# Low halves from GpSimd to VectorE, one activation kept in program order, and rotations issued by ScalarE, in a hybrid mLSTM and sparse-attention block

## The chip, the cores and the metric

The kernel runs on one core of one Trainium2 chip. The metric is the device time of one execution in microseconds (us); lower is better. The kernel before was timed in three runs with a median of 608.86 us.

## What is computed

One layer of a decoder block on 512 tokens of width 1024, in float32. The part of the reference that the change touches:

```
hN = _rmsnorm(x, norm_g[l])
p = _split_in(hN @ w_in[l])
...
kc = _compress(kvh(p["n_kc"]), cmp_pos_k[l], cmp_w1_k[l], cmp_w2_k[l])
vc = _compress(kvh(p["n_vc"]), cmp_pos_v[l], cmp_w1_v[l], cmp_w2_v[l])
ks = _partial_rope(kvh(p["n_ks"]), positions).transpose(0, 2, 1, 3)
kw = _partial_rope(kvh(p["n_kw"]), positions).transpose(0, 2, 1, 3)
...
return jax.nn.gelu(blocks @ w1) @ w2
```

The last line is the end of `_compress`. The queries are rotated with `_partial_rope` too. Behind this come an attention over 8 heads with three branches, the mLSTM over 4 heads, gates, two branch projections, an output projection, a residual sum and a final norm.

## The kernel before

Matrix products run in float32 precision as three passes on TensorE: each operand is split into a high half (a rounded copy, mostly made by ScalarE) and a low half (the operand minus the high half, mostly made by VectorE), and high times high, high times low and low times high are summed in PSUM. Names that end in `h` and `l`, or `hi` and `lo`, are such halves. So every weight that arrives costs a ScalarE copy (`wh<-wr`) and a VectorE subtraction (`wl<-wr,wh`) before the third pass of its product can start.

The stages that matter here, in order of time:

1. **Keys** (to 28 us). Raw columns of x (`xc`) times the weights of four key and value projections, into four PSUM banks (`keys_in`, L484). Beside it the norm's factor is worked out (`rs`) and spread over a tile `rB`.
2. **Small projection** (28 to 44 us). For each of 8 row blocks k, `normed_raw` (L509) makes the normed columns in place (`xc<-xc,rB`, VectorE), ScalarE makes the high half `hTh`, and `normed_low` (L512) makes the low half `hTl` (VectorE). `small(i)` (L504) makes the halves `shi` (ScalarE) and `slo` (GpSimd, `pool` in the code) of the narrow weights `sraw`, two row blocks at a time. TensorE takes, for each k, 12 matmuls of 288 columns (L624), of which the last four need `hTl` of that k; 96 in all. After the fourth k, the four key and value sums are moved out of PSUM (`kc`, `vc`, `ks`, `kw`), and the rotations of `ks` and `kw` are sent.
3. **Streamed jobs** (44 to about 90 us). A `Stream` feeds TensorE with jobs: gate projections, query projections (24 matmuls of 512 columns each, L230, L232, L234) and the first layers of the compression (8 matmuls, L277). Raw weights sit in three buffers `wr`; the next load is issued when a buffer has been split. In between come `keys(b)` (L344), which rotates the keys of branch b and makes their halves; `blocks(i)` (L719), which lays the keys and values out for the compression (tiles `Z`); `hidden(i)` (L739), the compression's activation, a chain of two small matmuls, a copy `ua` on ScalarE, four small VectorE steps, a tanh on ScalarE (`ub<-ub`) and two VectorE steps that end in `u`; and `compress_k`, whose matmul (L758) needs `u`.
4. **Attention** (about 90 to 230 us), with streamed jobs between the scores, then the mLSTM and the projections.

A rotation swaps 8-row strips of a tile into `rot`, by four small DMAs of 8 x 512 (`rotate`, L317 to L320). The keys' two rotations are issued by SyncE and GpSimd, the four of the queries (`rope_a`, L689) by SyncE, in `turned`, which the stream calls when the next job begins.

The order on the engines comes from two places. Where `ordered` names an engine (`act`, `dve`, `pool`), its instructions stay as the program issues them; elsewhere a scheduler of the framework places them. In stages 1 and 2 `act` and `dve` are ordered; `hidden` is not. Each engine executes its own list strictly in order, so an instruction that waits holds up all behind it.

Of the kernel before, what the change touches and what calls it, by code (L numbers as in the profile page):

```python
# [11 lines left out]
F32 = mybir.dt.float32  # L12
F32R = mybir.dt.float32r
I32 = mybir.dt.int32
AF = mybir.ActivationFunctionType
OP = mybir.AluOpType
AX = mybir.AxisListType.X

T = 512
# [70 lines left out]
def build(  # L90
# [3 lines left out]
    nc = tc.nc  # L94
    ordered = {"act", "dve"}

    class Engine:
# [15 lines left out]
    act, dve, pool = (  # L113
        Engine(e, n) for e, n in ((nc.scalar, "act"), (nc.vector, "dve"), (nc.gpsimd, "pool"))
    )
    A = act.activation
# [13 lines left out]
    def f(ap):  # L130
        return ap.bitcast(F32)
# [55 lines left out]
    class Stream:  # L187
# [27 lines left out]
        def run(self, jobs=1):  # L215
            for _ in range(jobs):
                self.step(1)
                while self.cur is not None:
                    self.step(1)
# [69 lines left out]
    prm = cst[:, CEND:CPOS].rearrange("p (c n) -> p c n", c=8)  # L289
# [16 lines left out]
    rpp = rp.__enter__()  # L306
# [10 lines left out]
    def rotate(rot, r, queue):  # L317
        for o in (0, 64):
            queue.dma_start(rot[o : o + 8], r[o + 8 : o + 16])
            queue.dma_start(rot[o + 8 : o + 16], r[o : o + 8])  # L320
# [3 lines left out]
    def turn_keys(b):  # L324
        rotate(turned_keys[b], kv[2 + b], nc.gpsimd if b else nc.sync)
# [9 lines left out]
    away, kv = {}, {}  # L335
# [8 lines left out]
    def keys(b):  # L344
        k = kv[2 + b]
        dve.tensor_tensor(k, k, Ct, OP.mult)
        rope_b(k, turned_keys[b])
        for g in range(2):
            s = slice(g * 64, g * 64 + 64)
            kh, kl = KK[g][0][s, b], KK[g][1][s, b]  # L350
            A(kh, k[s], AF.Copy)
            pool.tensor_tensor(kl, k[s], f(kh), OP.subtract)
        for g in range(2 * b):
            s = slice(g * 64, g * 64 + 64)
            o = slice((1 - g) * 64, (1 - g) * 64 + 64)
            for t in KK[g]:
                doubled.append(lambda t=t, o=o, s=s: nc.sync.dma_start(f(t[o]), f(t[s])))
# [18 lines left out]
    with tc.tile_pool(name="small", bufs=1, side="right") as sp, tc.tile_pool(  # L376
        name="ph0", bufs=2, side="right"
# [5 lines left out]
        raw = sp.tile([128, ND, SW], F32, name="sraw")  # L383
        shi = sp.tile([128, ND, SW], F32R, name="shi")
        slo = sp.tile([128, ND, SW], F32R, name="slo")
# [9 lines left out]
        rB = rpp.tile([128, T], F32, name="rB", tag="z", bufs=1)  # L395
# [59 lines left out]
        def x_low(k):  # L455
            dve.scalar_tensor_tensor(xl[k], xv[k], gv[k], f(xh[k]), OP.mult, OP.subtract)
# [11 lines left out]
        keys_in = [PP(), PP(), PP(), PO()]  # L468

        def kv_step(k):  # L470
            a, b = wh[k // 2][:, k % 2], wl[k // 2][:, k % 2]
            todo = [(p, c) for p in range(3) for c in range(4)]
            if k == 5:
                todo.insert(6, None)
            if k == ND - 1:
                todo = [(p, c) for c in range(4) for p in range(3)]
            for what in todo:
                if what is None:
                    factors()
                    continue  # L480
                p, c = what
                cs_ = slice(c * 128, c * 128 + 128)
                pin(
                    pe.matmul(  # L484
                        keys_in[c], (b if p == 2 else a)[:, cs_], xl[k] if p == 1 else xh[k],
                        start=k == 0 and p == 0, stop=k == ND - 1 and p == 2,
                    )
                )
# [12 lines left out]
            x_low(k)  # L501
            w_low(k // 2, slice(k % 2, k % 2 + 1), dve if k > 1 else pool)

        def small(i):  # L504
            ks = slice(2 * i, 2 * i + 2)
            A(shi[:, ks], raw[:, ks], AF.Copy)
            pool.tensor_tensor(slo[:, ks], raw[:, ks], f(shi[:, ks]), OP.subtract)

        def normed_raw(k):  # L509
            dve.scalar_tensor_tensor(xv[k], xv[k], gv[k], rB, OP.mult, OP.mult)  # L510
# [1 line left out]
        def normed_low(k):  # L512
            dve.tensor_tensor(hTl[:, k], xv[k], f(hTh[:, k]), OP.subtract)
# [21 lines left out]
        def sines():  # L535
            A(sc, ang, AF.Sin)
            for j, (i, sign) in enumerate(((1, 1.0), (1, 1.0), (0, -1.0), (0, 1.0))):
                pool.tensor_scalar(turned4[:, j], sc[:, i], sign, 1.0, OP.mult, OP.mult)
            nc.sync.dma_start(table.rearrange("j p t -> p j t"), turned4)
            turns4 = table.rearrange("j (f g) t -> (j f) (g t)", f=8)  # L540
            for dst, o in ((Ct, 0), (St, 16)):
                for g in (0, 64):
                    nc.sync.dma_start(dst[g : g + 16], turns4[o : o + 16])
# [41 lines left out]
        x_low(6)  # L585
        w_low(3)
        kv_step(5)
        A(rB, pr, AF.Copy)
        x_high(7)
        act.preload_act_table_set("silu_and_others")  # L590
        sines()
        normed_raw(0)
        x_low(7)
        kv_step(6)
        kv_step(7)

        for k in range(ND):
            if k < 4:
                small(k)
            A(hTh[:, k], xv[k], AF.Copy)  # L600
            if k < ND - 1:
                normed_raw(k + 1)
            normed_low(k)
            if k == 3:
                dve.tensor_scalar(prm[:, :, 10], prm[:, :, 10], 0.5, None, OP.mult)
                for c, (n, tag, bufs) in enumerate(
                    (("kc", "slt", 1), ("vc", "rw", 1), ("ks", "Th0", 2), ("kw", "Th1", 2))
                ):
                    kv[c] = rpp.tile([128, T], F32, name=n, tag=tag, bufs=bufs)
                    dve.tensor_tensor(kv[c], keys_in[c], rB, OP.mult)  # L610
                    if c > 1:
                        turn_keys(c - 2)
        stream.ahead = 1
        stream.fetch()
        stream.ahead = 2
        for b in range(2):
            keys(b)
        accs = [PS(), PS(), PT(), PT()]

        def project(k, tb, p):  # L620
# [68 lines left out]
    def rope_a(ps, name):  # L689
        r = rpp.tile([128, T], F32, name="rw", tag="rw", bufs=1)  # L690
        a = rpp.tile([128, T], F32, name="ra", tag="ra")
        A(r, ps, AF.Copy)
        dve.tensor_tensor(a, ps, Ct, OP.mult)
        rot = ropes.popleft()
        hl = [rpp.tile([128, T], F32R, name="r" + n, tag="r" + n) for n in "hl"]
        split(ps, *hl)

        def turned():
            rotate(rot, r, nc.sync)
            roped[name] = *hl, a, rot  # L700

        stream.then.append(turned)

    cmp_pool = tc.tile_pool(name="cmp", bufs=1, side="right")
# [14 lines left out]
    def blocks(i):  # L719
        z, parts = Z[i], []  # L720
        for g in range(2):
            for p in range(2):
                src = kv[i][g * 64 : g * 64 + 64, :].rearrange("p (n j b) -> p j n b", n=32, b=2)
                parts.append((src[:, :, :, p], *(z[p * 64 : p * 64 + 64, 0, :, l, g] for l in range(2))))
        for src, hi, lo in parts:
            A(hi, src, AF.Copy)
        for src, hi, lo in parts:
            dve.tensor_tensor(lo, src, f(hi), OP.subtract)
        rows = z.rearrange("p c j l g n -> p c (j l g) n")
        A(rows[:, 1, :, 0:31], f(rows[:, 0, :, 1:32]), AF.Copy)  # L730
        for c in range(2):
            o = i * 16 + c * 8
            for g in range(2):
                A(
                    z[:, c, :, :, g, 31].rearrange("p j l -> p l j"), f(cpos2[:, :, o : o + 8]),
                    AF.Copy,
                )

    def hidden(i):  # L739
        ph = PS()  # L740
        pe.matmul(ph[:, :64], first[i][:, 0], both, start=True, stop=False)
        pe.matmul(ph[:, :64], first[i][:, 1], both, start=False, stop=True)
        u0 = cp.tile([128, 64], F32, name="ua", tag="ua")
        u = cp.tile([128, 64], F32, name=f"u{i}")
        u2 = cp.tile([128, 64], F32, name="ub", tag="ub")
        A(u0, ph[:, :64], AF.Copy)
        dve.tensor_scalar(u, u0, u0[:, 31:32], None, OP.add)
        dve.tensor_tensor(u2, u, u, OP.mult)
        dve.tensor_scalar(u2, u2, 0.044715, 1.0, OP.mult, OP.add)
        dve.tensor_tensor(u2, u2, u, OP.mult)  # L750
        A(u2, u2, AF.Tanh, scale=float(np.sqrt(2 / np.pi)))
        dve.tensor_scalar(u2, u2, 0.5, 0.5, OP.mult, OP.add)
        dve.tensor_tensor(u, u, u2, OP.mult)
        return u
# [187 lines left out]
    A(gates, gp[:, :, 0:24], AF.Tanh, scale=0.5)  # L942
    pool.tensor_scalar(gates, gates, 0.5, 0.5, OP.mult, OP.add)
    run()
    run()
    stream.step(1)
    stream.ahead = 3
# [2 lines left out]
    for _ in log_forget():  # L950
        stream.step(1)
    stream.step(5)
    u0 = hidden(0)
    stream.step(8)
    stream.then.extend(doubled)
    stream.run(2)
# [5 lines left out]
    for_head(0)  # L962
    for_head(1)
    ordered.clear()
    u1 = hidden(1)
    stream.step(14)
    compress_v(u1)
    trig_pool.__exit__(None, None, None)
# [180 lines left out]
    n = 0  # L1149
# [403 lines left out]
    for h in range(4):  # L1553
# [5 lines left out]
        for sb in range(NT):  # L1559
            o, n = KOFF[sb], 512 - sb * 128  # L1560
# [41 lines left out]
        r = rsqrt(mp, va, NT, "rl")  # L1602
# [342 lines left out]
```

## Time and profile before

| what | value |
|---|---|
| median of 3 runs | 608.86 us (607.76 to 609.02) |
| profiled execution, time | 608.19 us |
| profiled execution, span from first to last instruction | 606.4 us |
| TensorE busy | 587.8 us (97%) |
| VectorE busy | 462.2 us (76%) |
| ScalarE busy | 363.7 us (60%) |
| GpSimd busy | 128.0 us (21%) |
| DMA moved | 129.52 MB, mean 214 GB/s |

In the views, PE is TensorE, PEld its weight load, DVE is VectorE, ACT is ScalarE, POOL is GpSimd and SPq is SyncE's queue. A row of the timeline gives the start, the duration, the engine, the line, the operation, the output and inputs, and in brackets how long the engine had been idle and what ended that. Ends of matmuls are modelled, so a wait of TensorE is best read from the starts. In a row of the windows, each engine's busy time is followed by its number of instructions in brackets; PEclk is the TensorE clock that was granted, as a share of full speed. L105 is the line of a helper through which nearly all VectorE, ScalarE and GpSimd instructions pass.

### The profile page before, as it was taken

How to read it: one execution, taken by the hardware profiler on the slowest of the kernel's cores; microseconds unless marked ns; L12 is line 12 of the kernel's file. 1: busy time of each engine (PE TensorE's matmuls, PEld its weight loads, DVE VectorE, ACT ScalarE, POOL GpSimd, SP SyncE). 2: the span in 40 equal slices, each digit the busy share in tenths (PEclk: the TensorE clock that was granted, in tenths of full speed). 3: DMA queues.
4: the chain of work that ended last, by engine and by line, in shares of the span. 5: the costliest groups of instructions: out<-in, count | busy, mean ns of one | idle time of the engine just before them, and what ended most of it. 6: DMA issues, size and time to landing. Idle time of an engine off the chain costs nothing.

```text
span 606.4 us, 8551 instructions
## 1 busy us (share of the span) xinstructions
PE 587.8 (97%) x2896; PEld 491.9 (81%) x2896; DVE 462.2 (76%) x855; ACT 363.7 (60%) x662; POOL 128.0 (21%) x204
## 2 busy tenths in 40 slices
PE   9989979998999999999999999999999999999995
PEld 6887768877878888888888888888888888888884
DVE  4799669867778778777999745869777766679885
ACT  6747755656657666665766666565756542644544
POOL 5634052335314534250000000000200010001011
PEclk9999989999999999999999999999999999999999
DMA  8936962876994799489684456699995697867723
GB/s 320 329 96 197 260 172 76 265 159 129 259 324 139 172 200 240 140 211 225 206 273 143 138 168 185 181 310 332 300 269 181 218 249 247 294 199 253 249 98 140
DMA packets 102484, 129.52 MB, mean 214 GB/s; under 512 B 6052, under 2 KB 63012, under 8 KB 102312
## 3 DMA queue, kind: packets, MB, share of 16 engines
q1 hardware_dynamic: 96392, 113.83, 59.3%
q0 software_dynamic: 5760, 14.75, 14.1%
q8 instruction: 23, 0.38, 0.3%
q10 hardware_dynamic: 288, 0.39, 0.2%
q14 instruction: 21, 0.17, 0.1%
HBM read 110.66 MB, written 42.02 MB: 252 GB/s over the span
## 4 chain that ended last, share of the span: by engine, by line
PE 79%; DVE 8%; ACT 5%; DMA 5%; issue 1%; SPq 1%; DVEq 0%; ACTq 0%
PE pp L232 11%; PE pp L234 10%; PE pp L230 10%; PE pp L1331 3%; PE pp L1333 3%; PE pp L1335 3%; PE pt L1069 2%; PE pp L484 2%; PE pt L1333 2%; PE pt L1335 2%; PE pt L1331 2%; PE pp L1673 2%; PE pp L1669 2%; PE pp L1671 2%; PE po L1081 1%
## 5 line engine op out<-in xcount | busy, mean ns | idle before, releaser
L105 DVE TENSOR_TENSOR wl<-wr,wh 128x1024 fp32r<-128x1024 f32 (+3 forms) x105 | 125.2, 1192 | 53.3 <-ACT wh L105 52.0
L105 ACT ACTIVATE wh<-wr 128x1024 fp32r<-128x1024 f32 (+3 forms) x106 | 108.0, 1021 | 79.1 <-PE pp L232 24.6
L234 PE MATMUL pp<-hTh,wl 128*128 128x512 f32 x320 | 126.6, 396 | 0.4 <-DVE wl L105 0.4
L232 PE MATMUL pp<-hTl,wh 128*128 128x512 f32 x320 | 126.5, 395 | 0.0
L230 PE MATMUL pp<-hTh,wh 128*128 128x512 f32 x320 | 126.2, 394 | 0.0
L105 POOL TENSOR_SCALAR P<-P,st,gates 128x128 f32<-128x128 f32 (+2 forms) x80 | 52.6, 681 | 107.1 <-DVE st L105 95.7
L234 PEld LDWEIGHTS pp<-hTh,wl 128*128 128x128 f32 x320 | 60.4, 189 | 12.7 <-DVE wl L105 1.2
L230 PEld LDWEIGHTS pp<-hTh,wh 128*128 128x128 f32 x320 | 60.5, 189 | 11.3
L232 PEld LDWEIGHTS pp<-hTl,wh 128*128 128x128 f32 x320 | 60.5, 189 | 11.2
L105 ACT ACTIVATE P<-P,st 128x128 f32<-128x128 f32 (+3 forms) x64 | 35.7, 559 | 31.3 <-DVE st L105 30.7
L105 POOL TENSOR_TENSOR rlr<-va,mhalf 128x4 f32<-128x4 f32 x4 | 4.1, 1034 | 222.3 <-ACT Dm L105 150.6
L105 DVE SCALAR_TENSOR_TENSOR u<-pp,cst,u 128x511 f32<-128x511 f32 (+2 forms) x48 | 35.6, 741 | 5.7 <-ACT u L105 5.5
L105 DVE CUSTOM_DVE_ANT_0 P<-ps,cst 128x128 f32<-128x128 f32 (+3 forms) x64 | 30.0, 478 | 8.0 <-PE ps L1050 5.8
L105 DVE TENSOR_TENSOR ptl<-pt,pth 128x384 fp32r<-128x384 f32 (+1 forms) x48 | 28.4, 592 | 5.7 <-ACT pth L105 5.7
L105 ACT ACTIVATE pth<-pt 128x384 fp32r<-128x384 f32 (+1 forms) x48 | 25.0, 520 | 11.9 <-PE pt L1069 11.4
L1069 PE MATMUL pt<-cst,P 128*128 128x128 f32 x160 | 25.6, 273 | 1.6 <-DVE ptl L105 1.6
L1069 PEld LDWEIGHTS pt<-cst,P 128*128 128x128 f32 x160 | 19.9, 140 | 6.1 <-DVE ptl L105 2.6
L1080 PE MATMUL po<-pth,vsw 128*128 128x512 f32 (+1 forms) x64 | 21.8, 350 | 0.7 <-DVE oc L105 0.7
L1081 PE MATMUL po<-ptl,vsw 128*128 128x512 f32 (+1 forms) x64 | 19.3, 328 | 0.0
L1335 PE MATMUL pp<-wh,S 128*128 128x512 f32 x48 | 18.7, 389 | 0.0
L1331 PE MATMUL pt<-wh,S 128*128 128x512 f32 x48 | 18.7, 389 | 0.0
L1333 PE MATMUL pt<-wl,S 128*128 128x512 f32 x48 | 18.7, 389 | 0.0
(429 smaller groups left out, 1415.6 us busy)
## 6 DMA issues: line engine op xcount, KB each, us to landing
wr<-w_in SPq DMA_DIRECT2D x62, 512.0 KB
qk<-hl SPq DMA_DIRECT2D x16, 512.0 KB
qk<-qk SPq DMA_DIRECT2D x16, 512.0 KB
wsumv<-w_in SPq DMA_DIRECT2D x4, 1024.0 KB
away<-s SPq DMA_DIRECT2D x16, 256.0 KB
wsumz<-w_in SPq DMA_DIRECT2D x4, 1024.0 KB
wsumout<-w_out SPq DMA_DIRECT2D x4, 1024.0 KB
wr<-wsumv SPq DMA_DIRECT2D x8, 512.0 KB
```

Of the source, the lines that this page charges most:

```text
L105: ins = fn(*args, **kw)
L230: pe.matmul(ps, a, c, start=k == 0, stop=False)
L232: pe.matmul(ps, a, d, start=False, stop=False)
L234: pe.matmul(ps, b, c, start=False, stop=k == nk - 1)
L484: pe.matmul(keys_in[c], (b if p == 2 else a)[:, cs_], xl[k] if p == 1 else xh[k], start=k == 0 and p == 0, stop=k == ND - 1 and p == 2,)
L1069: pe.transpose(pt[:, n : n + 128], P[:, POFF[qb] + kb * 128 : POFF[qb] + kb * 128 + 128], ident)
L1080: pe.matmul(po[:, kb * 128 :], vl, th, start=b == 0 and kb == 0, stop=False)
L1081: pe.matmul(po[:, kb * 128 :], vl, tl, start=False, stop=False)
L1331: pe.matmul(ps, a, c, start=begin, stop=False, skip_group_check=not first)
L1333: pe.matmul(ps, a, d, start=False, stop=False, skip_group_check=not first)
L1335: pe.matmul(ps, b, c, start=False, stop=k == 3, skip_group_check=not first)
L1669: pe.matmul(ps, p, ya(k), start=k == 0, stop=False)
```

## The change

Four edits:

- **Low halves.** The four `slo` subtractions go from GpSimd to VectorE, each behind the normalizations of one row block (`small_low`); the `shi` copies move up by a block, the first ahead of `rB`. The four low halves of the keys (`kl` in `keys`) go from GpSimd to VectorE as well. The table load for the sines, and the sines, move behind the second `shi`.
- **Order of the keys.** `ks` and `kw` are moved out of PSUM after row block 3 as before, `kc` and `vc` only after the loop (`keys_out`). `keys(1)` moves behind the first streamed job.
- **Activation in order.** `hidden(0)` and `hidden(1)` are issued with `act` and `dve` ordered (`in_order`).
- **Rotations of the queries.** `rope_a` calls `rotate` itself, on ScalarE's queue, instead of later on SyncE's.

```
             A(kh, k[s], AF.Copy)
-            pool.tensor_tensor(kl, k[s], f(kh), OP.subtract)
+            dve.tensor_tensor(kl, k[s], f(kh), OP.subtract)
...
-            pool.tensor_tensor(slo[:, ks], raw[:, ks], f(shi[:, ks]), OP.subtract)
...
+        def small_low(i):
+            dve.tensor_tensor(slo[:, pairs[i]], raw[:, pairs[i]], f(shi[:, pairs[i]]), OP.subtract)
...
+        small_high(0)
         A(rB, pr, AF.Copy)
         x_high(7)
-        act.preload_act_table_set("silu_and_others")
-        sines()
         normed_raw(0)
         x_low(7)
+        small_low(0)
...
+        def keys_out(c):
+            n, tag, bufs = (("kc", "slt", 1), ("vc", "rw", 1), ("ks", "Th0", 2), ("kw", "Th1", 2))[c]
+            kv[c] = rpp.tile([128, T], F32, name=n, tag=tag, bufs=bufs)
+            dve.tensor_tensor(kv[c], keys_in[c], rB, OP.mult)
+            if c > 1:
+                turn_keys(c - 2)
...
         for k in range(ND):
-            if k < 4:
-                small(k)
             A(hTh[:, k], xv[k], AF.Copy)
+            if k < 3:
+                small_high(k + 1)
+            if k == 0:
+                act.preload_act_table_set("silu_and_others")
+                sines()
             if k < ND - 1:
                 normed_raw(k + 1)
             normed_low(k)
+            if k < 3:
+                small_low(k + 1)
             if k == 3:
...
+                keys_out(2)
+                keys_out(3)
...
-        for b in range(2):
-            keys(b)
+        keys_out(0)
+        keys_out(1)
+        keys(0)
...
         def turned():
-            rotate(rot, r, nc.sync)
             roped[name] = *hl, a, rot
 
+        rotate(rot, r, nc.scalar)
         stream.then.append(turned)
...
+    def in_order(fn, *args):
+        ordered.update({"act", "dve"})
+        out = fn(*args)
+        ordered.clear()
+        return out
...
     run()
+    keys(1)
     run()
...
-    u0 = hidden(0)
+    u0 = in_order(hidden, 0)
...
-    u1 = hidden(1)
+    u1 = in_order(hidden, 1)
```

VectorE's list at the start of the small projection; `Th_143` is the last low half of x for the keys, and the rest are named above:

```order
 L105 SCALAR_TENSOR_TENSOR xc<-xc,rB 128x512
 L105 SCALAR_TENSOR_TENSOR Th_143<-xc,k_111 128x512
+L105 TENSOR_TENSOR slo<-sraw,shi 128x576
 L105 SCALAR_TENSOR_TENSOR xc<-xc,rB 128x512
 L105 TENSOR_TENSOR hTl<-xc,hTh 128x512
+L105 TENSOR_TENSOR slo<-sraw,shi 128x576
 L105 SCALAR_TENSOR_TENSOR xc<-xc,rB 128x512
 L105 TENSOR_TENSOR hTl<-xc,hTh 128x512
```

A `slo` now stands ahead of each of the second to fifth `xc<-xc,rB`. GpSimd's list loses its four.

ScalarE's list at the first activation of the compression; `ft` belongs to the forget gate, `s` to a gate job, `wh` are the high halves of the weights of coming jobs, `h` is the second first-layer sum, `KC` the compressed keys, `Th` the halves of the rotated queries. Numbers tell the `wh` apart:

```order
 L105 ACTIVATE ft_792<-ft_792 128x16
-L105 ACTIVATE wh_866<-wr_864 128x1024
 L105 ACTIVATE ua_840<-ps_837 128x64
+L105 ACTIVATE ub_842<-ub_842 128x64
 L105 ACTIVATE wh_886<-wr_884 128x1024
-L105 ACTIVATE ub_842<-ub_842 128x64
 L105 ACTIVATE s_861<-pp_802 128x512
 L105 ACTIVATE wh_912<-wr_910 128x1024
-L105 ACTIVATE Th_921<-ra_717 64x512
 L105 ACTIVATE h_898<-ps_875 128x256
```

The tanh `ub` now stands directly behind `ua`, ahead of `wh_886`; `wh_866` has moved up, ahead of this piece. On VectorE the subtraction for `wh_886` likewise moved from ahead of the last two steps of `u` to behind them.

ScalarE's list where the second query projection is moved out of PSUM, early in the attention; `rw` is the tile that is rotated, `rh` its unrotated high half, `P` a softmax block:

```order
 L105 ACTIVATE rh<-pp 128x512
+L319 DMA rot_88<-rw 8x512
+L320 DMA rot_88<-rw 8x512
+L319 DMA rot_88<-rw 8x512
+L320 DMA rot_88<-rw 8x512
 L105 ACTIVATE P,st<-P,st 128x256
 L105 ACTIVATE sc<-sc 128x256
```

Four DMA issues now stand in ScalarE's list ahead of the next softmax block; SyncE's list loses the same four. For the third query projection they stand ahead of a `pth<-pt` copy, the high half of transposed probabilities, and for the fourth behind a `wh<-wr`.

More of the change, by code (lines that the diff above doesn't have):

```diff
@@ L502, in both_low, with small_high @@
             w_low(k // 2, slice(k % 2, k % 2 + 1), dve if k > 1 else pool)
-        def small(i):
-            ks = slice(2 * i, 2 * i + 2)
-            A(shi[:, ks], raw[:, ks], AF.Copy)
-            pool.tensor_tensor(slo[:, ks], raw[:, ks], f(shi[:, ks]), OP.subtract)
+        pairs = [slice(2 * i, 2 * i + 2) for i in range(4)]
+        def small_high(i):
+            A(shi[:, pairs[i]], raw[:, pairs[i]], AF.Copy)
+        def small_low(i):
+            dve.tensor_tensor(slo[:, pairs[i]], raw[:, pairs[i]], f(shi[:, pairs[i]]), OP.subtract)
         def normed_raw(k):
@@ L603, in build @@
             normed_low(k)
+            if k < 3:
+                small_low(k + 1)
             if k == 3:
[L605 to L612, printed above, removed]
+                keys_out(2)
+                keys_out(3)
+        dve.tensor_scalar(prm[:, :, 10], prm[:, :, 10], 0.5, None, OP.mult)
         stream.ahead = 1
```

## The prediction

> **What bounds the kernel now.** I read the page's busy times first. TensorE (PE) has work nearly all the time.
>
> ```profile
> PE 587.8 (97%) x2896; PEld 491.9 (81%) x2896; DVE 462.2 (76%) x855; ACT 363.7 (60%) x662; POOL 128.0 (21%) x204
> ```
>
> So a gain is a gap on PE that closes. The windows by stage show where the gaps are: the columns are length, busy time of PE, PEld, DVE, ACT and POOL, then the granted clock, the DMA share and GB/s.
>
> ```profile
> 28.20:43.90 15.70, 13.60 (x98) 13.02 (x97) 15.34 (x21) 7.21 (x10) 6.36 (x7) 1.00 0.38 105
> 43.90:60.00 16.10, 15.89 (x71) 12.86 (x70) 15.75 (x26) 12.15 (x27) 7.89 (x7) 1.00 0.66 187
> 60.00:72.00 12.00, 11.12 (x56) 8.91 (x55) 7.33 (x7) 9.01 (x16) 0.27 (x1) 1.00 0.90 243
> 72.00:85.00 13.00, 9.78 (x49) 8.33 (x48) 9.93 (x20) 7.52 (x16) 8.74 (x21) 0.87 0.99 275
> ...
> 350.00:600.00 250.00, 249.45 (x1210) 210.30 (x1208) 181.75 (x332) 138.44 (x231) 17.13 (x23) 1.00 0.74 231
> ```
>
> From 350 to 600 us PE lacks 0.55 us. The early stages lack 2.10, 0.21, 0.88 and 3.22, and in the fourth the clock fell too: a mean of 0.87 over 13 us is 13 x 0.13 = 1.7 us of lost work. In the first two VectorE is busy 98% of the time; in the last two the DMA engines are. The timeline of PE shows each gap, with the matmul ahead of it:
>
> ```profile
> 28.41 0.43 PE L624 MATMUL ps<-shi,hTh 128*128 128x288 f32 x2
> ...
> 33.51 0.54 PE L624 MATMUL ps<-shi,hTl 128*128 128x288 f32 x2 [0.57 <-DVE hTl L105]
> ...
> 38.50 0.53 PE L624 MATMUL ps<-shi,hTl 128*128 128x288 f32 x2 [1.53 <-DVE hTl L105]
> ...
> 41.01 0.43 PE L624 MATMUL pt<-shi,hTh 128*128 128x288 f32 x2
> 41.28 0.43 PE L624 MATMUL ps<-slo,hTh 128*128 128x288 f32 x2
> ...
> 43.95 0.39 PE L230 MATMUL pp<-hTh,wh 128*128 128x512 f32 x1
> ...
> 55.06 0.39 PE L232 MATMUL pp<-hTl,wh 128*128 128x512 f32 x1
> 55.66 0.50 PE L234 MATMUL pp<-hTh,wl 128*128 128x512 f32 x1 [0.21 <-DVE wl L105]
> ...
> 60.55 0.39 PE L234 MATMUL pp<-hTh,wl 128*128 128x512 f32 x1
> 61.65 1.19 PE L277 MATMUL ps<-ws,Z 128*128 128x256 f32 x8 [0.71 <-PE pp L234]
> ...
> 62.91 0.40 PE L232 MATMUL pp<-hTl,wh 128*128 128x512 f32 x1
> 63.47 0.50 PE L234 MATMUL pp<-hTh,wl 128*128 128x512 f32 x1 [0.17 <-DVE wl L105]
> ...
> 77.44 0.40 PE L230 MATMUL pp<-hTh,wh 128*128 128x512 f32 x1
> 81.06 0.51 PE L758 MATMUL ps<-u,w2t 128*128 128x64 f32 x2 [3.22 <-ACT wh L105]
> ```
>
> Measured by starts: two L624 take 41.28 - 41.01 = 0.27, so 96 take 13.0 and the small projection, begun at 28.41, could end at 41.4; it ended at 43.95, **2.6** late. From 43.95 to 55.06 stand 49 matmuls of 512 columns, 0.227 each. By that pace 55.66 should be 55.29 (**0.4** lost), 61.65 should be 60.78 (**0.9**), 63.47 should be 63.14 (**0.3**), and 81.06 should be 77.67 (**3.4**). With the clock's **1.7** this is 9.3 us, all that the four edits aim at.
>
> **Low halves on VectorE.** The first rows are VectorE's, ScalarE's and GpSimd's in the small projection, the last two the `Z` halves with GpSimd at work on the keys' low halves, and without.
>
> ```profile
> 21.77 0.60 ACT L105 ACTIVATE rB<-pt 128x512 f32<-128x512 f32 x1 [0.84 <-PE pt L495]
> ...
> 23.00 1.28 ACT L105 ACT_TABLE_LOAD   x1
> ...
> 24.46 0.67 ACT L105 ACTIVATE shi<-sraw 128x576 fp32r<-128x576 f32 x1
> ```
>
> ```profile
> 25.35 6.95 POOL L105 TENSOR_TENSOR slo<-sraw,shi 128x576 fp32r<-128x576 f32 x4
> ```
>
> ```profile
> 25.68 1.65 DVE L105 TENSOR_TENSOR hTl<-xc,hTh 128x512 fp32r<-128x512 f32 x1 [1.19 <-ACT hTh L105]
> ...
> 30.95 1.91 DVE L105 SCALAR_TENSOR_TENSOR xc<-xc,rB 128x512 f32<-128x512 f32 x1
> 32.77 0.68 DVE L105 TENSOR_TENSOR hTl<-xc,hTh 128x512 fp32r<-128x512 f32 x1
> 33.38 0.74 DVE L105 SCALAR_TENSOR_TENSOR xc<-xc,rB 128x512 f32<-128x512 f32 x1
> ...
> 49.86 4.49 DVE L105 TENSOR_TENSOR Z<-kc,Z 64x256 fp32r<-64x256 f32 x3
> ...
> 58.02 1.85 DVE L105 TENSOR_TENSOR Z<-vc,Z 64x256 fp32r<-64x256 f32 x3
> ```
>
> While GpSimd computes (25.35 to 32.30), VectorE's steps, two kinds in turn from 25.68 to 32.77, take 1.65 to 1.91 instead of 0.68 and 0.74; once it has ended they are fast. The four cost about 4 x 1.1 = 4.5 us more than alone, the three `Z` 2.6 more. Taken over, the work costs VectorE four `slo` of 0.68 x 576/512 = 0.77 and four key halves of about 0.68, together 5.8: less than the 7.1 set free, and the 1.19 us wait for `hTh` is filled by a `slo`.
>
> Is the last `hTl` in time? After `rB` (ends 22.37) VectorE has 8 x 0.74 + 8 x 0.68 + 4 x 0.77, two moves and one low half of x at 0.7 each: 16.5, so 38.9 at the most. PE, unstalled, wants it about 1.5 us ahead of 41.4. It is about 1 us early, so all 2.6 come. The table load and sines lie beside VectorE's work: the `hTh` behind them would be ready at about 26.4 (23.0, then `hTh` and `shi` at 0.7 each, 1.28, the short sines and its own 0.7), when VectorE is still on the second `slo`. The first `shi` costs nothing if its weights have landed by 20.9: 0.67 fits into the 0.84 of idle time ahead of `rB`; if it is late, up to 0.7 comes back. `kc` now leaves PSUM only behind the loop and one `wl`, at 38.9 + 1.2 + 0.7 = 40.8 at the latest; the first L230 writes into that bank at 41.4, so this too is covered, by 0.6. The sine table's transfer goes out behind a 1 MB sum transfer; its cover is `wl`, `kc` and `vc`, which VectorE now does ahead of the first use.
>
> The `wl` of 55.66 comes forward by 4.5 + 2.6 + 1.2, and by 2.0 for three steps of the second branch's keys that now follow it, less four `slo` and two key halves, 4.5: 5.8 in all, while PE comes only 2.6 earlier. The 0.4, and the 0.9 and 0.3 queued behind it, go. The second branch's keys, 10 us later than before, are first read in the attention, near 88 us; the streamed jobs between cover them.
>
> By the Trainium skill (SBUF — State Buffer, section "SBUF: two separate sides") the pair of ports that VectorE and GpSimd share is an exclusive lock held for a whole instruction; the slow steps above agree. But Perfetto Trace Analysis (section "Optimizing Scalar/DVE Operations") warns that moving work between the two might not help, which by its words would leave the 2.6 where it was; here the slowed steps outweigh the moved ones.
>
> **Activation in order.** The gap at 81.06 has this chain (ScalarE, VectorE, SyncE, and the second activation's last step):
>
> ```profile
> 78.25 1.06 ACT L105 ACTIVATE wh<-wr 128x1024 fp32r<-128x1024 f32 x1 [2.53 <-DMA wr<-w_in]
> ...
> 79.21 0.24 ACT L105 ACTIVATE ub<-ub 128x64 f32<-128x64 f32 x1
> ```
>
> ```profile
> 79.34 1.23 DVE L105 TENSOR_TENSOR wl<-wr,wh 128x1024 fp32r<-128x1024 f32 x1 [1.54 <-ACT wh L105]
> ...
> 80.73 0.23 DVE L105 TENSOR_TENSOR u<-u,ub 128x64 f32<-128x64 f32 x1
> ...
> 86.31 0.22 DVE L105 TENSOR_TENSOR u<-u,ub 128x64 f32<-128x64 f32 x1
> ```
>
> ```profile
> 72.00 3.07 SPq L170 DMA_DIRECT2D wr<-w_in  x2
> ```
>
> The tanh stood behind a weight copy that waited for DMA, and the last steps of `u` behind the same weights' low half. Now both stand ahead; the 3.4 goes, and with it the 1.7 of clock, as gaps of 1.53 left the clock at 1.00 above.
>
> By the Trainium skill (TensorE: Matmul & The Clock Gate, section "What's actually happening") the clock halves after an idle window of about 3.4 us. The trace shows it after 3.22.
>
> What is late next: the second activation needs `h`, still behind that `wh` and one more on ScalarE. Its weights took from 72.00 to 78.25 to arrive, with the DMA engines 99% busy. PE reaches that point 4.2 us earlier (2.6 + 0.4 + 0.9 + 0.3), plus the 3.4. If the weights land just 4.2 earlier, about 74.0, two copies (1.06 each), `s` and `h` put `h` at 77, and PE, there at 74.6, waits 2.3; if their load speeds up with its earlier buffers, nothing. I take **1.5**. The second `u` was ready at 86.5; its chain now stands behind all the key and query halves, while PE gives it 15 matmuls, 3.4 us: 0 to 1.5, I take **0.9**. The first `u`, with table load and weight copies ahead: 0 to 0.8, I take **0.4**. Together 2.8 come back.
>
> **Rotations on ScalarE.** The third query's rotation, and ScalarE's next idle time:
>
> ```profile
> 122.26 0.71 SPq L319 DMA_DIRECT2D rot<-rw  x1
> ```
>
> ```profile
> 130.88 0.69 DVE L105 TENSOR_TENSOR rot<-rot,St 128x512 f32<-128x512 f32 x1 [4.52 <-DMA rot<-rw]
> ```
>
> ```profile
> 132.81 0.62 ACT L105 ACTIVATE P<-P,st 128x384 f32<-128x384 f32 x1 [3.11 <-DVE st L105]
> ```
>
> An issue takes ScalarE about as long as SyncE, 0.7, so 2.6 to 2.8 per rotation; softmax copies queue behind. ScalarE's idle time of 3.11 covers it. VectorE's wait of 4.52 is landing, not issue, and I leave it: 0, between a gain of 0.6 and a loss of 1.1 (where a weight copy of 1.06 now stands ahead).
>
> By the Trainium skill (DMA: Bandwidth & Descriptors, section "Issuing engines are not separate DMA queues") issuing elsewhere saves only the sequencer's time; no row here tests that yet.
>
> **The sum.** 9.3 - 2.8 = 6.5 us. The profiled execution took 608.19 (a span of 606.4 and 1.8 around it), so 601.7; the median of the runs, 608.86, lies 0.7 higher: **602.4**.
>
> **Rivals.**
>
> - A, *no new waits*: the weights land early; all 9.3 come: 599.6. For it: DMA is only 38% and 66% busy from 28 to 60. Against: 0.99 later. 0.18.
> - B, *DMA holds the third stage*: what PE gains by `u` it waits for `h`, and the clock falls again. Only 4.2 stay: 604.7. For it: 0.90 and 0.99 DMA share, and `wh` ended by DMA. 0.27.
> - C, *ScalarE's issues uncovered in the attention* (slower): three rotations hold the softmax 2.6 each and PE starves; with a fall of the clock of 1.7 behind each, 12.9, so 602.4 + 12.9 = 615.3. It decides once over half of that reaches PE. Against: 3.11 idle. 0.06.
> - D, *the slow steps are not GpSimd's doing* (slower): VectorE gets 5.8 more and no relief, PE waits some 2.7 longer for `hTl` and 1.2 for `wl`; 2.6 and 1.6 are not gained: 602.4 + 8.1 = 610.5. Against: they end with GpSimd's work. 0.04. This is also the warning quoted above, carried through.
>
> The forecast has 0.45. The **range** runs from 599.0 (A, less the 0.6) to 605.8 (B, plus the 1.1); C and D lie outside. 0.2%, 1.2 us, is about what a measurement of this kernel can tell from no change: faster 0.89 (forecast, A and nearly all of B), same 0.03, slower 0.08.
>
> **What would show it.** In the profile after: `hTl` and `xc` at 0.68 and 0.74 throughout; no L624 gap, the first L230 near 41.4; L758 within 1 us of the matmul ahead; clock 1.00 from 60 to 85; `h` or the second `u` as the last PE gap, 1 to 2 us; attention gaps as before. I am wrong if the slow steps stay, if the clock still falls, or if PE waits for ScalarE behind the rotations.

## The result

The changed kernel took 604.31 us (median of 8 runs, 603.26 to 606.09), the kernel before beside it 608.94 us (8 runs, 606.89 to 612.53). The ratio is 0.9925, with a 95% interval of 0.9900 to 0.9951: 4.6 us faster. Forecast was 602.4, in a range of 599.0 to 605.8, and 6.5 us of gain. A second set of runs gave 604.25 us and a ratio of 0.9904 (0.9885 to 0.9923). The size was nearly right. Where the time came from was not: the experiments show that the low halves, with the new order of the keys, bring all of it, and that the other two parts of the change bring nothing that can be told.

The profiled execution took 606.0 us (span 603.9). It is one of the longest of its eight; that of before took 608.19 (606.4).

### The profile page after: what moved, and what is told of

It is laid out like the page before. It is cut to its first block, busy times and chain, and to the rows that moved or that the text cites. A ratio compares the mean times of both kernels' runs of the same rounds, so it can differ in the third digit from the quotient of the medians.

```text
span 603.9 us, 8539 instructions
## 1 busy us (share of the span) xinstructions
PE 587.4 (97%) x2896; PEld 491.6 (81%) x2896; DVE 459.5 (76%) x863; ACT 365.0 (60%) x662; POOL 121.7 (20%) x196
## 4 chain that ended last, share of the span: by engine, by line
PE 46%; DVE 4%; DMA 2%; issue 1%; ACT 1%; DVEq 0%; ACTq 0%
PE pp L230 5%; PE pp L234 5%; PE pp L232 5%; PE pp L1351 2%; PE pp L1349 2%; PE pp L1353 2%; PE pp L1689 2%; PE pp L1687 2%; PE pp L1691 2%; PE pt L1353 1%; PE pt L1351 1%; PE pt L1349 1%; DVE wl L105 1%; DVE r L105 1%; DMA F<-w_in 1%
## 5 line engine op out<-in xcount | busy, mean ns | idle before, releaser
L230 PE MATMUL pp<-hTh,wh 128*128 128x512 f32 x320 | 126.4, 395 | 0.0
L105 POOL TENSOR_SCALAR P<-P,st,gates 128x128 f32<-128x128 f32 (+2 forms) x80 | 54.3, 699 | 102.6 <-DVE st L105 95.0
L230 PEld LDWEIGHTS pp<-hTh,wh 128*128 128x128 f32 x320 | 60.6, 189 | 11.4
L1087 PE MATMUL pt<-cst,P 128*128 128x128 f32 x160 | 25.5, 273 | 1.1 <-DVE ptl L105 1.1
L1087 PEld LDWEIGHTS pt<-cst,P 128*128 128x128 f32 x160 | 19.9, 140 | 5.4 <-issue 1.4
L1351 PE MATMUL pp<-wl,S 128*128 128x512 f32 x48 | 18.8, 392 | 0.1
L105 ACT ACTIVATE th<-u 128x512 f32<-128x512 f32 x16 | 10.1, 631 | 14.3 <-DVE u L105 12.4
```

What stands on the lines that cost most here:

```text
L105: ins = fn(*args, **kw)
L230: pe.matmul(ps, a, c, start=k == 0, stop=False)
L1087: pe.transpose(pt[:, n : n + 128], P[:, POFF[qb] + kb * 128 : POFF[qb] + kb * 128 + 128], ident)
L1351: pe.matmul(ps, a, d, start=False, stop=False, skip_group_check=not first)
```

## The profile after

The page's busy times, to be read against those of before:

```profile
PE 587.4 (97%) x2896; PEld 491.6 (81%) x2896; DVE 459.5 (76%) x863; ACT 365.0 (60%) x662; POOL 121.7 (20%) x196
```

VectorE has eight instructions more and is 2.7 us less busy; GpSimd has lost 6.3 us. The windows by stage (length, PE, PEld, DVE, ACT, POOL, granted clock, DMA share, GB/s):

```profile
28.20:41.30 13.10, 13.10 (x99) 13.03 (x98) 12.38 (x21) 6.19 (x9) 5.76 (x7) 1.00 0.50 147
41.30:57.00 15.70, 14.23 (x63) 11.47 (x63) 14.66 (x29) 13.90 (x30) 1.87 (x3) 1.00 0.55 169
57.00:70.00 13.00, 13.00 (x66) 10.79 (x64) 7.57 (x9) 5.53 (x7) 0.00 (x0) 1.00 1.07 260
70.00:82.00 12.00, 7.84 (x44) 6.46 (x44) 8.00 (x17) 9.02 (x19) 6.95 (x17) 0.96 0.81 212
```

The small projection now runs without a wait. Behind it PE lacks 1.47 us in the second row and 4.16 in the fourth, 5.63 us in all; before, the three stages behind the small projection lacked 0.21, 0.88 and 3.22, which is 4.31. The same in PE's timeline. The small projection is L635 now (L624 before), the activation's first matmuls are L758 and L759 (L741 and L742), and the matmuls that need `u` are L775 (L758) and L789.

```profile
28.46 0.43 PE L635 MATMUL ps<-shi,hTh 128*128 128x288 f32 x2
...
41.26 0.39 PE L230 MATMUL pp<-hTh,wh 128*128 128x512 f32 x1
...
54.23 0.50 PE L234 MATMUL pp<-hTh,wl 128*128 128x512 f32 x1 [1.47 <-DVE wl L105]
59.36 1.12 PE L277 MATMUL ps<-ws,Z 128*128 128x256 f32 x8
...
72.23 0.41 PE L758 MATMUL ps<-both,h 128*128 128x64 f32 x2 [2.13 <-ACT ft L105]
77.36 0.41 PE L775 MATMUL ps<-u,w2t 128*128 128x64 f32 x2 [0.23 <-issue]
80.56 0.43 PE L758 MATMUL ps<-both,h 128*128 128x64 f32 x2 [1.80 <-ACT h L105]
```

L230 starts 2.7 us earlier than the 43.95 of before. The wait of 3.22 ahead of the matmul that needs `u` is gone. In its place stand three others: for the third `wl`, and twice for `h`. In the small projection VectorE is fast, and it is GpSimd that is slow (VectorE's rows first, then GpSimd's):

```profile
25.13 0.68 DVE L105 TENSOR_TENSOR hTl<-xc,hTh 128x512 fp32r<-128x512 f32 x1
25.73 0.75 DVE L105 TENSOR_TENSOR slo<-sraw,shi 128x576 fp32r<-128x576 f32 x1
26.40 0.74 DVE L105 SCALAR_TENSOR_TENSOR xc<-xc,rB 128x512 f32<-128x512 f32 x1
```

```profile
26.10 5.59 POOL L105 TENSOR_SCALAR turned<-sc 128x32 f32<-128x32 f32 x4 [7.00 <-ACT sc L105]
```

## The experiments

Unless said otherwise each starts from the changed kernel and is timed in five rounds beside the kernel before, on the same chip. A result is the median, and the ratio to before with its 95% interval.

### The low halves back on GpSimd

The new order of the loop stays; only the engine changes.

```
-            dve.tensor_tensor(kl, k[s], f(kh), OP.subtract)
+            pool.tensor_tensor(kl, k[s], f(kh), OP.subtract)
...
-            dve.tensor_tensor(slo[:, pairs[i]], ...
+            pool.tensor_tensor(slo[:, pairs[i]], ...
```

> The changed kernel with the four `slo` and the four key halves back on GpSimd; the new order of the loop, the activation's order and ScalarE's issues stay. If GpSimd's work beside it is what slows VectorE, `hTl` and `xc` take 1.6 to 1.9 us again while GpSimd computes `slo`, PE waits 2 to 3 us in the small projection, and the time is 604.3 + 2.7 to 4 = 607.0 to 608.3. If the new order of the loop did it and not the engine, the steps stay at 0.7, and the time at 604.3 within 0.7.

Measured: 609.15 us, ratio 1.0004 (0.9992 to 1.0016). The whole gain is gone, and more than was expected. GpSimd's row, and VectorE's beside it:

```profile
28.98 5.60 POOL L105 TENSOR_TENSOR slo<-sraw,shi 128x576 fp32r<-128x576 f32 x3
```

```profile
29.52 1.92 DVE L105 TENSOR_TENSOR hTl<-xc,hTh 128x512 fp32r<-128x512 f32 x1
31.36 1.92 DVE L105 SCALAR_TENSOR_TENSOR xc<-xc,rB 128x512 f32<-128x512 f32 x1
33.21 1.92 DVE L105 TENSOR_TENSOR hTl<-xc,hTh 128x512 fp32r<-128x512 f32 x1
...
36.90 0.68 DVE L105 TENSOR_TENSOR hTl<-xc,hTh 128x512 fp32r<-128x512 f32 x1
```

Between 28.98 and 34.58 three of VectorE's steps take 1.92 us; right behind, they take 0.68 again. So GpSimd's work is the cause of the slow steps. And with the activation still in order and the rotations still on ScalarE, the large wait for `u` is back:

```profile
84.73 0.41 PE L775 MATMUL ps<-u,w2t 128*128 128x64 f32 x2 [3.67 <-ACT h L105]
```

So the order of the activation is not what took that wait away. It binds the steps of `hidden` to each other, and not the weight copies, which the scheduler still puts between them: here a `wh` from 81.19 to 82.25 ahead of the tanh.

In this profile PE does not wait in the small projection at all: it takes 12.95 us to the first L230, against 12.80 in the changed kernel. (Everything up to there is 1.7 us late, because the first matmuls of this execution ran at half pace until about 10 us, where the changed kernel's were at full pace by 8: at 8.98 three of them take 1.48 us, there 0.85.) What PE loses by the halves shows behind: it waits 7.68 us from 41 to 90 (5.63 in the changed kernel), and there is a second fall of the clock at 140.

### Only the small weights' low halves back on GpSimd

> The changed kernel with only the four `slo` back on GpSimd; the key halves stay on VectorE. If the small projection's wait (2.6 us of the sum) and what hangs on it are the gain of the low halves, the time is 606.5 to 608. If the key halves carry as much, it is 605 to 606; if the new loop's order suffices for `slo`, 604.3 within 0.7.

Measured: 607.59 us, ratio 0.9975 (0.9955 to 0.9994). The four `slo` are worth 3.3 us of the 4.8, by these medians, and the key halves the rest. PE's waits:

```profile
36.97 0.54 PE L635 MATMUL ps<-shi,hTl 128*128 128x288 f32 x2 [0.61 <-DVE hTl L105]
...
74.50 0.66 PE L758 MATMUL ps<-both,h 128*128 128x64 f32 x2 [5.02 <-ACT ft L105]
84.54 0.41 PE L775 MATMUL ps<-u,w2t 128*128 128x64 f32 x2 [2.23 <-ACT h L105]
```

The first L230 starts at 42.41, only 1.1 us later than in the changed kernel and 1.5 earlier than in the kernel before. The rest comes later, as longer waits for `h` and `u` and as 10.2 us at half clock (3.4 in the changed kernel's profile over the same stage). A likely reason, not tested apart, is that what delays VectorE early delays the release of weight buffers, and so the loads behind them.

### The activation left to the scheduler

```
-    u0 = in_order(hidden, 0)
+    u0 = hidden(0)
...
-    u1 = in_order(hidden, 1)
+    u1 = hidden(1)
```

> The changed kernel with both calls of the activation left to the scheduler again. If the order is what took the `u` gap away, the tanh or the last steps of `u` stand behind a weight copy again, PE waits about 2 to 3 us more at L775, and the time is 606 to 608. If the weights' transfers hold this stage whatever the order, PE waits as long elsewhere, and the time stays at 604.3 within 0.8.

Measured: 605.51 us, ratio 0.9935 (0.9921 to 0.9949). The interval overlaps that of the changed kernel, and the time lies between the two that were expected. The wait for `u` is 0.68 us, where 2 to 3 more were expected:

```profile
71.66 0.41 PE L758 MATMUL ps<-both,h 128*128 128x64 f32 x2 [1.67 <-ACT ft L105]
77.62 0.41 PE L775 MATMUL ps<-u,w2t 128*128 128x64 f32 x2 [0.68 <-ACT ub L105]
80.05 0.53 PE L758 MATMUL ps<-both,h 128*128 128x64 f32 x2 [1.03 <-ACT h L105]
```

### The rotations back on SyncE

```
+            rotate(rot, r, nc.sync)
             roped[name] = *hl, a, rot
 
-        rotate(rot, r, nc.scalar)
```

> The changed kernel with the queries' rotations issued by SyncE at the start of the next job, as before. The scheduler then puts `h` ahead of the next weight copy on ScalarE again. If ScalarE's issues are what put `h` behind that copy, the gap of 2.13 us ahead of the first L758 goes, and the time is 602.2 to 603.5. If the rotations' earlier issue is what the attention gained by (its gaps are 2.7 us after, 3.75 before), the time is 605 to 606. If neither, 604.3 within 0.7.

Measured: 603.89 us, ratio 0.9911 (0.9895 to 0.9926), not to be told from the changed kernel. But the mechanism shows. The first query's four issues stand on ScalarE from 62.42 to 65.70 us. ScalarE's rows around `h`, in the changed kernel:

```profile
70.27 1.06 ACT L105 ACTIVATE wh<-wr 128x1024 fp32r<-128x1024 f32 x1 [3.41 <-DMA wr<-w_in]
...
71.71 0.38 ACT L105 ACTIVATE h<-ps 128x256 f32<-128x256 f32 x1
```

And with SyncE issuing the rotations:

```profile
66.18 0.58 ACT L105 ACTIVATE rh<-pp 128x512 fp32r<-128x512 f32 x1
...
67.13 0.39 ACT L105 ACTIVATE h<-ps 128x256 f32<-128x256 f32 x1
```

With the four issues on ScalarE the scheduler places the next weight copy ahead of `h`, and that copy waits for its transfer. Without them `h` comes 4.6 us earlier, and no wait for it is left at the first L758. PE then waits 1.29 us for the first `u` and 1.26 for the second.

### The low halves alone

The kernel before with the first two edits only: no `in_order`, and `rotate` on SyncE in `turned`.

> The kernel before with only the low halves on VectorE and the loop's new order: the activation is left to the scheduler and SyncE issues the rotations. If the low halves bring the whole gain, and the other two parts only move waits about, the time is 603.5 to 605 (0.991 to 0.994 of before). If the activation's order carries part of it, as the sum on record has it (3.4 of 9.3 us), the time is 606 or more.

Measured: 602.65 us, ratio 0.9888 (0.9857 to 0.9919); six of seven runs lie between 601.81 and 603.13, below both expected ranges. All of the gain is here. The profile is that of the seventh run (605.55). PE's waits between 41 and 90 us:

```profile
54.12 0.50 PE L234 MATMUL pp<-hTh,wl 128*128 128x512 f32 x1 [1.44 <-DVE wl L105]
...
75.84 0.41 PE L775 MATMUL ps<-u,w2t 128*128 128x64 f32 x2 [1.14 <-ACT h L105]
80.87 0.30 PE L789 MATMUL ps<-w2t,u 128*64 128x64 f32 x2 [0.44 <-issue]
85.55 0.36 PE L1067 MATMUL ps<-k,Th 128*128 128x256 f32 x1 [0.25 <-DVE VC L105]
```

They sum to 3.27 us, against 5.63 in the changed kernel's profile. (From 90 to 240 us this long run waits 5.10, against 2.70.) The unordered activation with ScalarE's rotations took 605.51, and the last experiment below, which is this kernel with one small move, 602.82 (0.9886 to 0.9914). The intervals of these two ratios don't meet, nor does that of the first one meet the interval above, so ScalarE's issues cost 2.7 us where the activation is not ordered. Ordering it on top gives that back in part (604.31), and alone it changes nothing that can be told (603.89).

### The raw weights' tile moved

```
-        raw = sp.tile([128, ND, SW], F32, name="sraw")
         shi = sp.tile([128, ND, SW], F32R, name="shi")
         slo = sp.tile([128, ND, SW], F32R, name="slo")
+        raw = sp.tile([128, ND, SW], F32, name="sraw")
```

> The changed kernel with the small weights' raw tile placed behind their two halves in memory; every engine's order is the same. If ScalarE's first copies into the compression's tiles (41.46, idle 1.95 for PE's last L635) wait because these tiles take the memory of `slo`, they now start near 39.6, the key halves and the third `wl` come up to 1.5 us earlier, and the gap of 1.47 us at 54.23 falls to 0.7 or less; time 603 to 604, less if the earlier weights help the later waits too. If VectorE's own work sets that `wl`, the gap stays over 1.2 and the time at 604.3 within 0.5.

Measured: 604.17 us, ratio 0.9924 (0.9908 to 0.9940): no difference, and the wait stays.

```profile
41.38 0.23 ACT L105 ACTIVATE cpos<-cst 128x32 fp32r<-128x32 f32 x1 [1.95 <-PE pt L635]
```

So either these tiles still share memory with what PE reads last, or the wait has another cause; this edit doesn't tell. PE's wait for the third `wl` is 1.45 us, as before the edit.

### The third low half early

The first query's job is made known early, and all three waiting weights are split ahead of the first branch's keys:

```
     gate_job(2)
+    cols(NQ, lambda ps: rope_a(ps, ("q", 0)))
...
         keys_out(1)
+        stream.ahead = 3
+        stream.fetch()
+        stream.ahead = 2
         keys(0)
...
-    queries(0)
```

> The changed kernel with the first query's weights split ahead of the first branch's keys: its `wl` (52.86 in the changed kernel, where PE waits 1.47 us for it) is done near 42.5. That `wl` also holds one of three raw buffers: the next load of the compression's weights goes out at 54.20, right behind it, and would now go out 10 us earlier, when the DMA engines are 55% busy. If the late `wl` is the cause of the new gaps, the 1.47 goes, `h` and `u` (2.13, 0.23 and 1.80) come earlier by 2 us or more in all, the clock stays at 1.00, and the time is 600 to 602. If the transfers of 57 to 70 us hold this stage by their number, PE waits for `h` what it no longer waits for `wl`: 603.5 to 604.5.

Measured: 603.77 us, ratio 0.9911 (0.9882 to 0.9940). The wait for `wl` is gone and PE is busy from 28 to 57 us without a gap. Then it waits, in one piece, for `h`:

```profile
72.77 0.66 PE L762 MATMUL ps<-both,h 128*128 128x64 f32 x2 [4.36 <-ACT ft L105]
```

(Behind the edit the lines stand three or four lower: L762 is the changed kernel's L758, L779 its L775, L1090 its L1087.) That is 0.8 more than the 1.47 and 2.13 together, and the clock is halved for 6.8 us with it. The load that was to go out 10 us earlier went out only 1.2 us earlier. SyncE's rows, with a sum's two transfers and the store ahead of it:

```profile
42.88 2.29 SPq L928 DMA_DIRECT2D wsumv<-w_in  x2
52.54 0.36 SPq L364 DMA_DIRECT2D away<-s  x1
53.00 0.38 SPq L266 DMA_DIRECT2D wr<-cmp_w_k  x1
```

The store waits for ScalarE's `s`, and the load stands behind it. The edit also had an effect that was not meant: both transfers of 1 MB start here, while in the changed kernel the first of them starts at 25.00.

### The third low half early, rotations on SyncE

> The early `wl` and the rotations issued by SyncE together. If the late `wl` and `h` behind a weight copy are two separate costs, this is the fastest: 598.5 to 601. If one takes the place of the other, as the early `wl` alone, within 0.7.

Measured: 604.66 us, ratio 0.9929 (0.9900 to 0.9957), slower than expected. `h` comes in time, and PE waits 3.91 us for `u`, at L779, instead, behind first-layer weights of which ScalarE had to wait 3.09 us for the transfer.

### Stores by GpSimd as well

The low halves alone, with the early split and

```
-            stream.then.append(lambda: nc.sync.dma_start(away[base, j], s))
+            stream.then.append(lambda: nc.gpsimd.dma_start(away[base, j], s))
```

> The low halves alone (602.65), with the first query's weights split early and the `away` stores issued by GpSimd instead of SyncE. With the early split alone, the next load of the compression's weights still went out at 53.00, since on SyncE it stood behind a store that waited for ScalarE's `s` until 51.9. If that queue holds the stage, the load now goes out near 44, into the time in which the DMA engines are little used, the first layers and `h` have their weights in time, no gap over 1 us is left between 41 and 85, the clock stays at 1.00, and the time is 599.5 to 601.5. If the transfers or the buffers hold it all the same, a gap of 3 us or more stands at L775 again, the clock falls with it, and the time is 602.5 to 604.5.

Measured: 610.25 us, ratio 1.0008 (0.9991 to 1.0024): 7.6 us slower than the low halves alone, outside both expectations. The load does go out early (45.40, instead of 54.10 there), `h` is ready at 66.26, and its first matmul doesn't wait. But SyncE's next load goes out at 56.51, and ScalarE's copy ahead of the second `h` waits 3.27 us for its transfer. PE's waits in the stage, and one in the attention:

```profile
78.17 0.69 PE L762 MATMUL ps<-both,h 128*128 128x64 f32 x2 [2.67 <-ACT h L105]
...
172.70 0.90 PE L1090 MATMUL pt<-cst,P 128*128 128x128 f32 x3 [4.11 <-DVE ptl L105]
```

The last has its cause in VectorE, which waits for a rotation issued by SyncE:

```profile
169.01 0.69 DVE L105 TENSOR_TENSOR rot<-rot,St 128x512 f32<-128x512 f32 x1 [7.49 <-DMA rot<-rw]
```

Each of the two long waits, 2.67 and 4.11, brings 6.8 us at half clock. So here rotations on SyncE hurt. The low halves alone show the same chain, smaller: in their profile VectorE waits 5.26 us for this rotation, PE 2.27 behind it, and the clock falls at 169.4. With the rotations back on SyncE in the changed kernel no such wait came in the execution profiled.

### Both edits in the changed kernel

> The changed kernel (activation in order, rotations issued by ScalarE) with the same two edits, early split and stores by GpSimd. If the two other parts of the change pay once the weights are in time, as the sum on record has it, it is as fast as the low halves with these edits or faster. If ScalarE's issues still put `h` behind a weight copy that waits for its transfer, PE waits over 2 us ahead of the first L758 and the time is 1 to 3 us above.

Measured: 606.79 us, ratio 0.9951 (0.9934 to 0.9967). With the rotations on ScalarE the wait at 172 is 0.97 us, but the first `h` stands behind a waiting weight copy again: 5.76 us ahead of L762. Neither of these two is a way forward. What they leave open is a kernel with the early split that keeps the first sum's transfer where it was; it wasn't tried.

### The changed kernel again

> The changed kernel itself, for a second interval beside the two below. 603.5 to 605; the low halves alone took 602.65 on another occasion, and if the other two parts cost something this stays 1 us or more above that.

Measured: 604.25 us, ratio 0.9904 (0.9885 to 0.9923). That is 1.6 above the low halves alone; the two intervals overlap, so a cost of the other two parts together is likely but not shown. Its profiled execution is a short one (602.2 us, span 600.2), and its waits in the same places are 1.46, 0.94, 0.24, 0.69, 0.95 and 0.41.

### The sine table's steps on ScalarE

The low halves alone, and

```
-                pool.tensor_scalar(turned4[:, j], sc[:, i], sign, 1.0, OP.mult, OP.mult)
+                A(turned4[:, j], sc[:, i], AF.Copy, scale=sign)
```

> The low halves alone, with the four small `turned` steps of the sine table on ScalarE instead of GpSimd; every other instruction stands where it stood. In the changed kernel they took GpSimd 5.59 us, beside VectorE's work, and 0.76 before. If sharing with VectorE is what stretches them, they take ScalarE about 0.8 to 1.0 us, the table's transfer goes out near 27 instead of 31.71, and the first wait for it (0.45 us on VectorE) goes; `hTl` and `xc` stay at 0.68 and 0.74, and a time of 602.0 to 603.3 says again that the low halves alone are faster than the whole change (604.3). If the low halves alone were only a good draw, this comes out at 604 to 605.

Measured: 602.82 us (601.6 to 603.2), ratio 0.9900 (0.9886 to 0.9914). The low halves alone were not a good draw. The four steps take 0.59 us:

```profile
26.15 0.59 ACT L105 ACTIVATE turned<-sc 128x32 f32<-128x32 f32 x4
```

The table's transfer goes out at 27.70, 4.0 us earlier, but the loads from it start at 34.00 (33.82 in the changed kernel), so VectorE's wait of 0.52 for the keys' rotation stays: that part of the expectation failed. The transfer stands behind a 1 MB sum transfer that goes out at 25.24; that this holds it was not tested.

## Why the prediction was right, and where it was not

**The small projection, 2.6 us.** The size is right: 2.7, with `hTl` and `xc` at 0.68 and 0.74 throughout. Rival D is refuted: with `slo` back on GpSimd the steps take 1.92 again. But the sum put all of the 2.6 down to the slow steps, and by these profiles that was too much. With `slo` on GpSimd and only the new order of the loop the first L230 stands at 42.41, so about 1.5 of the 2.7 us are gained without VectorE's relief, and the engine brings the other 1.2. A likely reason is that the wait of 1.53 before stood behind four moves out of PSUM as well (VectorE, 34.72 to 37.11), two of which now follow the loop; the order was not tested with the other parts left out. In time nothing of this is left without the low halves on VectorE: with the new order and the other two parts kept the ratio is 1.0004. The Trainium skill (Perfetto Trace Analysis, section "Optimizing Scalar/DVE Operations") warns that offloading operations between VectorE and GpSimd might not help. In this kernel it did help: the same changed kernel with the halves on VectorE gives 0.9925.

**The third `wl`, 0.4 us, and 0.9 and 0.3 behind it.** The step that failed is "comes forward by 4.5 + 2.6 + 1.2, and by 2.0 [...], less [...] 4.5: 5.8 in all". It came forward by 1.5. VectorE's row in the kernel before:

```profile
54.38 1.23 DVE L105 TENSOR_TENSOR wl<-wr,wh 128x1024 fp32r<-128x1024 f32 x1
55.52 0.42 DVE L105 TENSOR_TENSOR vsw<-ps,vsw 128x256 fp32r<-128x256 f32 x1
```

And in the changed kernel:

```profile
47.73 0.42 DVE L105 TENSOR_TENSOR vsw<-ps,vsw 128x256 fp32r<-128x256 f32 x1
...
50.36 2.47 DVE L105 TENSOR_TENSOR Z<-vc,Z 64x256 fp32r<-64x256 f32 x4
52.86 1.32 DVE L105 TENSOR_TENSOR wl<-wr,wh 128x1024 fp32r<-128x1024 f32 x1
```

The sum took VectorE's order behind the loop as unchanged but for one branch's keys. In fact the value halves `vsw`, the gates' sums and the second branch's `Z`, all behind that `wl` before, now stand ahead of it, some 5 us. PE came 2.7 us earlier and the `wl` 1.5, so PE's wait grew from 0.21 to 1.47. The 0.9 and the 0.3 did go.

**The activation in order, 3.4 us less 2.8.** The wait for `u` went, but not for the reason given. It stays away without the order (0.68, and 1.14 with the low halves alone), and it comes back with the order when the low halves are on GpSimd (3.67). The come-backs were sized at 1.5, 0.9 and 0.4. In the profiled execution the second `h` cost 1.80 and the two `u` 0.23 and nearly nothing; a wait of 2.13 for the first `h` was not forecast at all. Over the stage from 41 to 90 us PE waits 5.63 us in one profile of the changed kernel and 4.69 in the other, against 4.31 before: no gain in place of a net 2.2.

**The rotations, 0.** In the attention no loss came: the waits are 0.52, 1.13 and 1.05 us, 2.70 in all against 3.75 before, and rival C did not come. That these are shorter isn't shown to be the rotations' doing: with SyncE issuing them PE waits 2.47 us from 90 to 240. The forecast looked for their cost in the wrong place. Their issues changed where the scheduler puts a weight copy in the stage ahead, and there cost the wait for the first `h`.

**The clock, 1.7 us.** The size fits the mean; "1.00 from 60 to 85" does not come out. The profiled execution has the same fall as before, that of the second set has none:

```profile
80.00:85.00 5.00, 4.45 (x15) 3.63 (x16) 4.21 (x11) 2.89 (x10) 4.11 (x10) 0.66 0.91 256
```

```profile
70.00:85.00 15.00, 11.78 (x62) 9.41 (x63) 10.78 (x25) 9.15 (x23) 8.79 (x24) 1.00 0.83 225
```

The mean granted clock was 0.9956 over 14 runs of the changed kernel and 0.9922 over 60 of the kernel before; 0.0034 of 604 us is 2.1 us. This figure is rough. It is a mean over whole executions, so it doesn't say whether the falls that are missing were those of this stage. And each mean holds a fall behind the last matmul, which costs TensorE nothing: by its share of the clock 1.5 us in the profile before (0.57 over the last 3.4 us), 2.0 and 1.5 in the two of the changed kernel.

So 4.6 us is 2.7 of the small projection and, as far as the means tell, about 2 of the clock. The rest about cancels: PE waits 0.4 to 1.3 us more from 41 to 90 us, and 1.1 to 1.7 less from 90 to 240. The two profiled executions, with one fall each in the stage, bear this out: their spans differ by 2.5 us, which is about 2.7 less 1.3 plus 1.1.

That the measured time lies in the range is in part luck. Of the 6.5 us forecast, the net 2.2 of the stage behind the small projection did not come, and the range reached far enough for that because it ran to rival B. Rival B, the transfers, had 0.27, and its picture is the one that the profiled execution shows: PE waits for `h` what it gains by `u`, and the clock falls again. Its 604.7 is nearer to 604.31 than the forecast's 602.4, though its sum is not right either: it counts 1.6 us for waits for weights and nothing for the clock. How far transfers, the order on SyncE or the release of buffers hold that stage is not settled: the early split took the wait for `wl` away and brought a longer one, but it also moved a 1 MB transfer into that stage.

## What to carry to other kernels

Work that two engines can't do side by side is better put on one of them, as long as the steps that it slows cost more than the step itself. Ahead of a forecast, compare the whole order of each engine before and after, and not only around the lines that were edited: here a DMA issue on ScalarE moved a weight copy ahead of a copy that PE was waiting for, and with the keys moved back 5 us of other work stood ahead of a `wl`. Test the parts of a change one by one: two of the three parts here were worth nothing that could be told, or less, hidden under the gain of the first.

## What the runs showed of the hardware

- **GpSimd is slowed too.** The four `turned` steps take 0.76 us in the kernel before, 1.24 us with `slo` on GpSimd, and 5.59 us when VectorE works without a pause beside them (`hTl`, `slo` and `xc` in turn). On ScalarE they take 0.59.
- **The half clock comes in spells of 3.4 us.** Ahead of the last matmul, every fall in the profiles lasts 3.4 or 6.8 us at 0.50, so each spell costs 1.7 us. By the Trainium skill (TensorE: Matmul & The Clock Gate, section "What's actually happening") the clock is judged by free-running windows of about 3.4 us and falls after an idle one. The length agrees. But here no idle window was needed. With the activation unordered, PE was busy for half of the 3.4 us ahead of the fall:

```profile
77.00:80.40 3.40, 1.75 (x9) 1.25 (x9) 2.29 (x4) 3.21 (x8) 2.89 (x7) 0.98 0.86 249
80.40:83.80 3.40, 3.40 (x11) 2.78 (x11) 3.19 (x10) 1.75 (x5) 2.89 (x7) 0.52 0.92 238
```

In the changed kernel's second profile as little work brought no fall:

```profile
76.00:79.40 3.40, 1.76 (x10) 1.07 (x9) 2.13 (x5) 3.10 (x7) 2.81 (x8) 1.00 0.95 280
```

What tells them apart is where the waits lie. The falls of one profile start a whole number of 3.413 us apart: before, at 81.22 and, behind the last matmul, at 603.46, which is 153 of them. Counted back in such steps from its own last fall (597.26), the changed kernel's second profile has stretches from 75.02 to 78.43 and on to 81.85, and PE is busy for 2.60 and 2.49 us in them: the same waits, shared out over two. Over all fourteen profiles, with the stretches counted so from 41 to 185 us, each one at full clock with PE busy for 1.70 us or less was followed by a fall (12 of them), and of those with 1.76 or more only one (1.96, all low halves on GpSimd).

So in this kernel waits that add up to half of such a stretch can halve the clock in one execution and not in the next. Cutting one long wait into several is then no protection by itself.
